# Fewer, larger transfers for sample rows, attention outputs and weight sums, and a new planned order

## The chip, the cores and the metric

The kernel runs on one core of a Trainium2 chip. The metric is device time in microseconds: 773.1 us is the median of three runs of the kernel before (771.97 to 775.28). The engines are named as in the profile: PE is TensorE (matrix products; PEld are its weight loads), DVE is VectorE, ACT is ScalarE, POOL is GpSimd, and SP is the engine that issues the transfers (DMAs).

## The reference

One layer of a streaming encoder, for 1024 prompt rows and 32 sample rows of width 1024 that share the weights:

```python
# hn = RMSNorm_pre(h)
# [qA kA vA gA qB kB vB gB] = hn @ w_in             one projection, 1024 x 4096
# oA = chunked band attention (8 heads x 64), relative-position bias
#      each frame reads its own 64-frame chunk and the previous 8 chunks
# oB = stick-breaking attention (8 heads x 64), strictly causal
# y  = concat(oA * silu(gA), oB * silu(gB)) @ w_out
# h  = h + RMSNorm_post(y)
# h  = h + sigmoid(h @ w_ple_gate) * (p @ w_ple)
```

Besides the two results it returns the new keys and values of both attentions, for prompt and sample. The sample's attention reads 512 cached rows and its own 32. All is float32.

## The kernel before

**Staging.** After a start that norms and transposes the input, eight stages follow, one for each pair of heads (A0, B0, A1, B1 and so on, A band attention, B stick-breaking). In stage n the attention of pair n is woven with the projections of pair n+1, in the last one with the gates. The pairs A1, B1, A3 and B3 carry sample attention of four heads each (`sample_attention`). Then come the embedding's products, the output product and the gate product, the latter two by a Strassen-like scheme with seven products of half matrices, which needs sums of weight quarters T1 to T4. `sum_weights` prepares these sums inside the stages 2, 4, 5 and 6 (`SUMS_AT`): for each of `o` (w_out) and `g` (w_ple_gate) and each of four row blocks it loads four quarters of 128 x 512, subtracts and adds on POOL, and stores four sums to DRAM (`sum_dr`).

**Attention of a head.** For each of eight query blocks: scores on PE into PSUM, softmax or stick-breaking weights in two tiles (`om`, `be`), and a transpose of the weights. For most blocks PE does the transpose (`ptw`). For the blocks in `ROUND` (5 to 7 of a band head, 4 to 6 of a stick-breaking head) VectorE transposes 32 x 32 squares, one transfer writes them to DRAM (`swap`) and four read them back. The result is split in a high and a low part (`wTh`, `wTl`), and every four blocks `values` multiplies them with the values into one PSUM bank (`PV`). The bank's two halves of rows are added, in two pieces of 256 columns, each through a tile `ot` and with a transfer of its own to `o_dr`.

**Keys and values.** `keys_out` and `values_out` turn a projection's columns into rows, in squares of 32 x 32, and store them as outputs. The 32 sample rows are stored by `sample_rows`, in four transfers of 4 KB for each pair and kind. `vs_dr` holds the sample's new values in squares for `sample_attention`.

**Room.** `om` and `be` tiles and some others come out of one heap of 6880 columns (`heap`), which grants room in the order in which the tiles are written down. `ot` is a ring of three tiles of 256 columns, `sg` a ring of three tiles of 512, shared by weight sums, gates and later loads.

**Order.** Nothing is issued in the order of the source. A `Recorder` keeps all operations with their dependences; `simulate` plans them with a cost for each (`cost`), `latest` gives each a due time by a backward pass, and a last `simulate` ranks each engine's queue by due time plus a shift. The shifts are two tables, `AHEAD_OF` (by engine and tile name) and `AHEAD_AT` (by stage as well). The plan models transfers by constants, and in the kernel before it lets SP issue while the pieces of transfers under way stay below 1900:

```python
            elif e == "SP":
                while away and (away[0][0] <= t or flying + o.pieces > AWAY):
                    landed, pieces = heapq.heappop(away)
                    flying -= pieces
                    t = max(t, landed)
```

All instructions are emitted from line 780, so the profile tells them apart by tile names. Every transfer is issued by SP.

Of the kernel before, what the change touches and what calls it, by code (L numbers as in the profile page):

```python
# [13 lines left out]
P = 128  # L14
D = 1024
SEQ = 1024
NS = 32
# [11 lines left out]
    ('ACT', 'L'): -809, ('ACT', 'Qfs'): -495, ('ACT', 'S'): -671, ('ACT', 'be'): 45,  # L29
    ('ACT', 'gT'): 1145, ('ACT', 'junk'): -1222, ('ACT', 'o'): 225, ('ACT', 'oT'): -1406,  # L30
    ('ACT', 'om'): -82, ('ACT', 'ot'): -967, ('ACT', 'p'): -874, ('ACT', 'pleo'): -1053,
    ('ACT', 'sgg'): 65, ('ACT', 'stq'): -314, ('ACT', 'stv'): -824, ('ACT', 'v'): 55,
    ('ACT', 'wTh'): -117, ('ACT', 'whS'): 246, ('ACT', 'whs'): 933, ('ACT', 'x'): -696,
    ('ACT', 'xS'): -616, ('DVE', 'Kl'): -588, ('DVE', 'L'): 544, ('DVE', 'S'): -85,
    ('DVE', 'Vl'): -913, ('DVE', 'cc'): -493, ('DVE', 'diags'): -1253, ('DVE', 'g'): 212,
    ('DVE', 'h'): -1097, ('DVE', 'hnl'): 570, ('DVE', 'lg'): 343, ('DVE', 'om'): -53,
    ('DVE', 'ot'): -267, ('DVE', 'over'): 483, ('DVE', 'sgg'): -356, ('DVE', 'sq'): 277,
    ('DVE', 'stats'): -1190, ('DVE', 'uu'): 246, ('DVE', 'v'): -653, ('DVE', 'vx'): -722,
    ('DVE', 'w'): -1469, ('DVE', 'wTl'): 37, ('DVE', 'wl'): 652, ('DVE', 'wlS'): -1002,
# [3 lines left out]
    ('POOL', 'be'): 196, ('POOL', 'gT'): 309, ('POOL', 'o'): -123, ('POOL', 'ogg'): 890,  # L43
    ('POOL', 'om'): 197, ('POOL', 'rs'): -497, ('POOL', 's'): -1046, ('POOL', 'sgg'): 929,
# [4 lines left out]
}  # L49
AHEAD_AT = {  # L50
    (0, 'ACT', 'pleo'): 1195, (0, 'ACT', 'sq'): 1380, (0, 'ACT', 'stk'): -1095, (0, 'ACT', 'v'): 1160,
    (0, 'DVE', 'hnl'): -45, (0, 'DVE', 'rb'): 799, (0, 'DVE', 'sq'): 461, (0, 'DVE', 'x'): 572,
# [3 lines left out]
    (2, 'ACT', 'be'): -135, (2, 'ACT', 'om'): 146, (2, 'ACT', 'stk'): -313, (2, 'ACT', 'stv'): 933,  # L56
    (2, 'ACT', 'v'): -818, (2, 'ACT', 'wTh'): 315, (2, 'ACT', 'wh'): -172, (2, 'DVE', 'S'): 534,
    (2, 'DVE', 'om'): 779, (2, 'DVE', 'wTl'): -209, (2, 'PE', 'PV'): 241, (2, 'PE', 'S'): 63,
    (2, 'PE', 'mm'): 48, (2, 'PE', 'ptw'): 89, (2, 'POOL', 'be'): -1200, (2, 'SP', 'kl'): 504,
    (2, 'SP', 'swap'): 262, (3, 'ACT', 'be'): 80, (3, 'ACT', 'om'): 256, (3, 'ACT', 'stk'): 956,  # L60
    (3, 'ACT', 'wh'): -21, (3, 'ACT', 'whs'): -356, (3, 'DVE', 'om'): -326, (3, 'DVE', 'ot'): -819,
# [3 lines left out]
    (4, 'ACT', 'om'): -35, (4, 'ACT', 'wTh'): -365, (4, 'ACT', 'whs'): -1064, (4, 'DVE', 'S'): -89,  # L65
    (4, 'DVE', 'Ss'): 1254, (4, 'DVE', 'ot'): 307, (4, 'DVE', 'wTl'): -134, (4, 'PE', 'S'): 77,
    (4, 'PE', 'ptw'): 56, (4, 'PE', 'ptws'): -349, (4, 'POOL', 'ksS'): -959, (4, 'POOL', 'om'): 162,
    (4, 'POOL', 'w'): -151, (4, 'POOL', 'wl'): 1076, (4, 'SP', 'Kcs'): 477, (4, 'SP', 'be'): -112,
    (4, 'SP', 'o'): -577, (4, 'SP', 'wr'): -890, (5, 'ACT', 'be'): -546, (5, 'ACT', 'kd'): -484,
    (5, 'ACT', 'stk'): 1450, (5, 'ACT', 'wTh'): -482, (5, 'DVE', 'S'): -110, (5, 'DVE', 'om'): -127,  # L70
# [3 lines left out]
    (6, 'ACT', 'L'): 734, (6, 'ACT', 'be'): -459, (6, 'ACT', 'kd'): 409, (6, 'ACT', 'stv'): 1412,  # L74
# [4 lines left out]
    (7, 'ACT', 'om'): 64, (7, 'ACT', 'stk'): -573, (7, 'ACT', 'wTh'): -208, (7, 'DVE', 'Kcs'): 660,  # L79
# [6 lines left out]
    (8, 'POOL', 'ogg'): -1077, (8, 'POOL', 'om'): 190, (8, 'POOL', 'sgg'): -350, (8, 'POOL', 'w'): 324,  # L86
# [3 lines left out]
    (10, 'POOL', 'r'): 153, (11, 'DVE', ''): -1125, (11, 'DVE', 'lg'): 155, (11, 'DVE', 'lo'): 1476,  # L90
    (11, 'DVE', 'ug'): -230, (11, 'DVE', 'wl'): -51, (11, 'DVE', 'wlS'): 1328, (11, 'POOL', 'h'): -525,
    (11, 'POOL', 'ms'): -252, (12, 'DVE', 'S'): 224, (12, 'DVE', 'cc'): 571, (12, 'POOL', 'gT'): -1069,
# [163 lines left out]
PASSES = 1  # L256
# [158 lines left out]
class Recorder:  # L415
# [94 lines left out]
    def cost(eng, method, args, kw, writes, reads):  # L510
# [27 lines left out]
        for v in (out, args[1]):  # L538
            if isinstance(v, View) and v.buf.pool is not None:
                size, run = 4 * v.shape[0] * v.free(), 4 * v.shape[-1]  # L540
# [82 lines left out]
    def simulate(self, rank):  # L623
# [83 lines left out]
        out, port, line, table, away, flying, last = [], 0.0, 0.0, AF.Exp, [], 0, 0.0  # L707
        while len(out) < len(self.ops):
# [26 lines left out]
            elif e == "SP":  # L735
                while away and (away[0][0] <= t or flying + o.pieces > AWAY):
                    landed, pieces = heapq.heappop(away)
                    flying -= pieces
                    t = max(t, landed)
                free[e] = t + o.busy  # L740
                line = max(line, t + DMA_START) + o.late
                heapq.heappush(away, (line + DMA_DONE, o.pieces))
                flying += o.pieces
# [42 lines left out]
def stream_step(  # L786
# [1485 lines left out]
```

## Time and profile before

| | |
|---|---|
| median of three runs | 773.1 us |
| the profiled execution, its time | 773.43 us |
| its span, first to last instruction | 771.7 us |
| busy, share of the span | PE 98%, PEld 91%, DVE 79%, ACT 68%, POOL 58% |
| mean DMA rate | 225 GB/s |
| granted clock of PE | 1.00 |

The span lies inside the execution's time; the difference is what surrounds the program. A busy share is an average over stages with different limits, so it is read by stretches. PE's ends are modelled, and short gaps between products may not show as idle time.

### The profile page before, as it was taken

Reading aid. Unit: us, or ns where it says so; the run is one execution under the profiler, and the core shown is the slowest. Engines: PE = TensorE matmul, PEld = TensorE weight load, DVE = VectorE, ACT = ScalarE, POOL = GpSimd, SP = SyncE. Lnnn points to the kernel's source line nnn. Section 1 sums busy time; section 2 is a strip of 40 time slices with the busy share of each in tenths; the row PEclk is TensorE's granted clock in tenths of the full one; section 3 lists DMA queues with packets and bytes.
Section 4 is the critical chain, followed back from the end, with each engine's and each line's share of the span. In section 5 each row is a group of like instructions: output and inputs, shape, how many; then the busy total and the mean of one; then the engine's idle time right before and its main releaser. Section 6 shows DMA issues by size and latency. Waiting matters only on the chain.

```text
span 771.7 us, 14284 instructions
## 1 busy us (share of the span) xinstructions
PE 758.4 (98%) x4410; PEld 698.9 (91%) x4410; DVE 611.6 (79%) x1067; ACT 525.0 (68%) x1122; POOL 447.2 (58%) x503
## 2 busy tenths in 40 slices
PE   9999999999999999999999999999999999999997
PEld 7999999999989899999999999999998877888786
DVE  7837868878878898959898698698565688988965
ACT  6656776787766776866788586665347877884641
POOL 6624434751356682557874467679463448689533
PEclk9999999999999999999999999999999999999999
DMA  8658667476789858889799989897779866769664
GB/s 302 220 146 223 178 166 218 120 197 206 182 192 253 218 171 229 258 237 263 216 240 269 246 231 223 270 276 214 213 267 300 275 221 227 235 202 332 214 212 136
DMA packets 202333, 173.61 MB, mean 225 GB/s; under 512 B 66817, under 2 KB 164457, under 8 KB 202258
## 3 DMA queue, kind: packets, MB, share of 16 engines
q1 hardware_dynamic: 202258, 172.70, 77.1%
q8 instruction: 35, 0.57, 0.3%
q14 instruction: 40, 0.33, 0.1%
HBM read 105.46 MB, written 58.78 MB: 213 GB/s over the span
## 4 chain that ended last, share of the span: by engine, by line
PE 86%; DVE 4%; DMA 4%; SPq 3%; issue 1%; ACT 1%; DVEq 0%; POOL 0%; ACTq 0%; POOLq 0%
PE mm_gA L780 6%; PE mm_gB L780 6%; PE mm_kA L780 6%; PE mm_qA L780 5%; PE mm_kB L780 5%; PE mm_vA L780 5%; PE mm_qB L780 4%; PE PVB L780 4%; PE mm_vB L780 4%; PE SB L780 4%; PE PVA L780 3%; PE ple L780 3%; PE SA L780 3%; SPq L780 3%; PE g0P L780 3%; PE g2P L780 3%
## 5 line engine op out<-in xcount | busy, mean ns | idle before, releaser
L780 POOL TENSOR_TENSOR be<-be 128x128 f32<-128x128 f32 (+8 forms) x66 | 85.1, 1294 | 48.6 <-DVE be L780 23.0
L780 DVE TENSOR_TENSOR_SCAN be<-be,SB 128x384 f32<-128x384 f32 (+5 forms) x96 | 91.5, 963 | 8.2 <-ACT be L780 4.3
L780 ACT ACTIVATE be<-SB 128x384 f32<-128x384 f32 (+4 forms) x192 | 83.4, 497 | 18.2 <-DVE be L780 7.0
L780 DVE TENSOR_TENSOR wTl<-be,wTh 128x640 fp32r<-128x640 f32 (+2 forms) x48 | 51.9, 1086 | 11.2 <-ACT wTh L780 7.8
L780 ACT ACTIVATE be<-be,statA 128x640 f32<-128x640 f32 (+3 forms) x64 | 44.5, 696 | 11.6 <-DVE statA L780 11.5
L780 DVE STREAM_TRANSPOSE be<-be 128x640 f32<-128x640 f32 (+3 forms) x56 | 47.9, 866 | 3.4 <-POOL be L780 2.3
L780 ACT CAST wTh<-be 128x640 fp32r<-128x640 f32 (+2 forms) x48 | 37.6, 784 | 13.2 <-DMA be<-swapB 7.3
L780 PE MATMUL SB<-kdB,LB 128*128 128x384 f32 (+5 forms) x96 | 33.7, 354 | 0.4 <-issue 0.3
L780 PE MATMUL SB<-klB,LB 128*128 128x384 f32 (+5 forms) x96 | 33.3, 347 | 0.0
L780 DVE CUSTOM_DVE_ANT_0 be<-SA,biasA 128x320 f32<-128x320 f32 (+3 forms) x64 | 29.7, 481 | 4.4 <-PE SA L780 3.4
L780 POOL TENSOR_TENSOR gB<-gB,gB 128x256 f32<-128x256 f32 x32 | 26.9, 861 | 9.8 <-DMA gB<-in_w_ple_gate_dram 7.9
L780 ACT CAST wTh<-ptwB 128x512 fp32r<-128x512 f32 (+3 forms) x48 | 22.4, 484 | 13.0 <-PE PVB L780 8.0
L780 PE MATMUL SA<-kdA,LA 128*128 128x320 f32 (+2 forms) x96 | 30.3, 325 | 0.2 <-PE mm_kB L780 0.2
L780 PE MATMUL SA<-klA,LA 128*128 128x320 f32 (+2 forms) x96 | 30.1, 317 | 0.0
L780 POOL TENSOR_TENSOR oB<-oB,oB 128x256 f32<-128x256 f32 x32 | 25.6, 826 | 6.7 <-DMA oB<-in_w_out_dram 4.8
L780 PE MATMUL ptwB<-ident,be 128*128 128x128 f32 x144 | 26.5, 274 | 2.4 <-ACT be L780 1.0
L780 POOL TENSOR_TENSOR klB<-stkB,kdB 64x1024 fp32r<-64x1024 f32 x8 | 20.0, 2504 | 14.0 <-ACT kdB L780 12.1
L780 DVE TENSOR_TENSOR wTl<-ptwB,wTh 128x512 fp32r<-128x512 f32 (+3 forms) x48 | 25.0, 540 | 3.9 <-ACT wTh L780 3.7
L780 POOL TENSOR_TENSOR klA<-stkA,kdA 64x1024 fp32r<-64x1024 f32 (+2 forms) x9 | 19.3, 2150 | 14.4 <-ACT kdA L780 9.5
L780 DVE TENSOR_TENSOR wTl<-ptwA,wTh 128x128 fp32r<-128x128 f32 (+3 forms) x48 | 21.8, 478 | 5.3 <-ACT wTh L780 3.5
L780 DVE TENSOR_TENSOR LA<-stqA,LA 64x1024 fp32r<-64x1024 f32 (+2 forms) x9 | 15.6, 1730 | 11.9 <-ACT LA L780 11.8
L780 POOL TENSOR_TENSOR wl_vB<-wr_vB,wh_vB 128x512 fp32r<-128x512 f32 x8 | 10.5, 1309 | 24.5 <-DMA stvA<-swapA 13.3
(694 smaller groups left out, 2653.6 us busy)
## 6 DMA issues: line engine op xcount, KB each, us to landing
swapA<-be SPq DMA_DIRECT2D x24, 320.0 KB, 3.7
be<-swapA SPq DMA_DIRECT2D x96, 80.0 KB, 3.0
oB<-in_w_out_dram SPq DMA_DIRECT2D x16, 256.0 KB, 4.2
sum_dro<-oB SPq DMA_DIRECT2D x16, 256.0 KB, 3.2
gB<-in_w_ple_gate_dram SPq DMA_DIRECT2D x16, 256.0 KB, 3.9
sum_drg<-gB SPq DMA_DIRECT2D x16, 256.0 KB, 3.8
x<-in_x_prompt_dram SPq DMA_DIRECT2D x16, 256.0 KB, 3.9
h_dr<-h SPq DMA_DIRECT2D x8, 512.0 KB, 4.3
```

Source lines behind the costliest of these rows:

```text
L780: getattr(getattr(tc.nc, o.what[0]), o.what[1])(*args, **kw)
```

## The change

It does the following:

- **Sample rows.** `sample_rows` stores each pair's keys as one block of squares into DRAM (`ks_dr`; the values are in `vs_dr` already). Only at the last pair of each kind does one transfer, DRAM to DRAM, gather all four pairs into the output.
- **Attention's outputs.** One copy, one addition, one transfer of 512 columns instead of two of each with 256.
- **Weight sums.** Two loads of whole rows (128 x 1024) instead of four quarters, and two stores of two sums each; the order of the sums in `sum_dr` is changed so that each pair lies together.
- **Room.** `ot` becomes two tiles of 512 columns; Qh and Ql of sample attention share one. `sg` becomes a heap of 2048 columns. The attention heap shrinks from 6880 to 6112.
- **Order.** SP's model: the next transfer is issued when the eighth before it has landed. Other constants; four backward and forward passes instead of one; both shift tables replaced in full.

Transfers: 52 fewer for sample rows, 32 for attention's outputs, 32 for weight sums.

```diff
-    ('ACT', 'L'): -809, ('ACT', 'Qfs'): -495, ('ACT', 'S'): -671, ('ACT', 'be'): 45,
+    ('ACT', ''): -789, ('ACT', 'Qs'): 1305, ('ACT', 'be'): 7, ('ACT', 'gT'): -203,
...
-ISSUE = 550
+ISSUE = 480
-DMA_START, DMA_DONE, DMA_RATE, DMA_MARGIN = 1950, 300, 320.0, 2000
-AWAY = 1900
+DMA_START, DMA_DONE, DMA_RATE, DMA_MARGIN = 1850, 1600, 320.0, 2100
+LANES = 8
-PASSES = 1
+PASSES = 4
...
-                while away and (away[0][0] <= t or flying + o.pieces > AWAY):
-                    landed, pieces = heapq.heappop(away)
-                    flying -= pieces
-                    t = max(t, landed)
+                if len(landed) >= LANES:
+                    t = max(t, landed[-LANES])
...
+    ks_dr = {ab: scratch([4, P, NS], f"ks_dr{ab}") for ab in "AB"}
-    heap = Heap(rec, at, "be", 6880)
+    heap = Heap(rec, at, "be", 6112)
+    sgs = Heap(rec, at2, "sg", 2048)
...
-    def sample_rows(dst, squares):
-        for g in range(4):
-            later(dst[:, 32 * g:32 * g + 32], squares[32 * g:32 * g + 32])
+    def sample_rows(ab, p, dst, squares, dr):
+        if squares is not None:
+            later(dr[p], squares)
+        if p == 3:
+            src = dr.rearrange("p (g t) f -> (p g) t f", t=32)
+            later(dst[0, 0].rearrange("t (p x) d -> t (p x d)", p=4).rearrange("t (x f) -> x t f", f=32), src)
...
-            for x in range(2):
-                c = slice(2 * x * P, (2 * x + 2) * P)
-                ot = at.tile([P, 2 * P], F32, tag="ot", name=f"ot{nm}_{g}_{x}", bufs=3)
-                nc.scalar.copy(ot[r], acc[o, c])
-                rec.behind()
-                nc.vector.tensor_tensor(ot[r], acc[r, c], ot[r], ALU.add)
-                dma(o_dr[sidx(ab, p)][r, (4 * g + 2 * x) * P:(4 * g + 2 * x + 2) * P], ot[r])
+            ot = at.tile([P, 4 * P], F32, tag="ot", name=f"ot{nm}_{g}", bufs=2)
+            nc.scalar.copy(ot[r], acc[o])
+            rec.behind()
+            nc.vector.tensor_tensor(ot[r], acc[r], ot[r], ALU.add)
+            dma(o_dr[sidx(ab, p)][r, 4 * g * P:(4 * g + 4) * P], ot[r])
...
-        for key in ("B12", "B22", "B11", "B21"):
-            b[key] = at2.tile([P, 512], F32, tag="sg", name=f"{w}{key}{kt}", bufs=3)
-            rec.hold(b[key])
-            dma(b[key], weight_part(w, key, kt))
...
+        for x in range(2):
+            b = sgs.tile([P, 2, 512], f"{w}B{x}{kt}", F32)
+            rec.hold(b)
+            dma(b, weight_rows(w, 4 * x + kt).rearrange("p (n c) -> p n c", n=2))
+            rows.append((b[:, 0], b[:, 1], b))
+        (b11, b12, top), (b21, b22, low) = rows
+        sub(b22, b22, b12, ALU.subtract)
+        sub(b12, b12, b11, ALU.subtract)
+        sub(b11, b22, b11, ALU.add)
+        dma(sum_dr[w][kt, 0:2].rearrange("s p c -> p s c"), top)
+        sub(b21, b11, b21, ALU.subtract)
+        dma(sum_dr[w][kt, 2:4].rearrange("s p c -> p s c"), low)
```

More of the change, by code (lines that the diff above doesn't have):

```diff
@@ L44 @@
-    ('POOL', 'om'): 197, ('POOL', 'rs'): -497, ('POOL', 's'): -1046, ('POOL', 'sgg'): 929,
[4 rows of a table removed]
+    ('ACT', ''): -789, ('ACT', 'Qs'): 1305, ('ACT', 'be'): 7, ('ACT', 'gT'): -203,
+    ('ACT', 'hnh'): -1389, ('ACT', 'junk'): -898, ('ACT', 'kd'): 1122, ('ACT', 'newh'): -1293,
+    ('ACT', 'oT'): -414, ('ACT', 'ot'): -375, ('ACT', 'pleo'): -576, ('ACT', 'sq'): -123,
+    ('ACT', 'stk'): -620, ('ACT', 'stq'): -202, ('ACT', 'stv'): -542, ('ACT', 'v'): -52,
+    ('ACT', 'vt'): -1008, ('ACT', 'w'): 293, ('ACT', 'wTh'): 73, ('ACT', 'whS'): -255,
@@ L56 @@
[L56 to L61, printed above, removed]
[3 rows of a table removed]
@@ L65 @@
[L65 to L70, printed above, removed]
[3 rows of a table removed]
@@ L92 @@
-    (11, 'POOL', 'ms'): -252, (12, 'DVE', 'S'): 224, (12, 'DVE', 'cc'): 571, (12, 'POOL', 'gT'): -1069,
[4 rows of a table added]
+    (2, 'ACT', 'be'): -228, (2, 'ACT', 'wh'): 1095, (2, 'DVE', 'S'): -256, (2, 'DVE', 'wTl'): 48,
+    (3, 'ACT', 'Kh'): -747, (3, 'ACT', 'L'): -877, (3, 'ACT', 'stk'): 463, (3, 'ACT', 'v'): 1320,
[4 rows of a table added]
+    (4, 'ACT', 'v'): -124, (4, 'ACT', 'wTh'): 148, (4, 'DVE', 'S'): 35, (4, 'DVE', 'Vl'): 65,
[6 rows of a table added]
+    (6, 'ACT', 'stq'): -1082, (6, 'ACT', 'v'): -940, (6, 'ACT', 'wTh'): 245, (6, 'DVE', 'S'): 110,
+    (6, 'DVE', 'wTl'): -591, (6, 'PE', 'S'): -57, (6, 'POOL', 'be'): -98, (6, 'POOL', 'g'): -142,
@@ new lines @@
+    (6, 'POOL', 'kl'): 171, (6, 'POOL', 'om'): 174, (6, 'SP', 'wr'): 487, (7, 'ACT', 'L'): -205,
+    (7, 'ACT', 'om'): 566, (7, 'DVE', 'Vl'): 692, (7, 'DVE', 'diags'): -616, (7, 'DVE', 'om'): -105,
[4 rows of a table added]
+    (8, 'PE', 'ptw'): -685, (8, 'PE', 'ptxs'): 106, (8, 'POOL', 'ogg'): 307, (8, 'POOL', 'om'): 622,
+    (8, 'POOL', 'sgg'): -1299, (8, 'POOL', 'wl'): 308, (8, 'SP', 'Kcs'): -265, (8, 'SP', 'Vcs'): 639,
[3 rows of a table added]
+    (11, 'ACT', 'whS'): 739, (11, 'ACT', 'x'): -201, (11, 'ACT', 'xS'): -151, (11, 'DVE', 'S'): 1275,
[4 rows of a table added]
@@ L537, in cost @@
         size, run = 4, 0
-        for v in (out, args[1]):
-            if isinstance(v, View) and v.buf.pool is not None:
+        for v in (args[1], out):
+            if isinstance(v, View) and (v.buf.pool is not None or not run):
                 size, run = 4 * v.shape[0] * v.free(), 4 * v.shape[-1]
@@ L705, in leave @@
                 come(new.place, b.gone)
-        out, port, line, table, away, flying, last = [], 0.0, 0.0, AF.Exp, [], 0, 0.0
+        out, port, line, table, landed, last = [], 0.0, 0.0, AF.Exp, [], 0.0
         while len(out) < len(self.ops):
@@ L1071, in back @@
             later(o_p[0, 0, :, h2, :].rearrange("(b p) h d -> p b (h d)", p=P), out[:, b0:8, :])
-            sample_rows(o_s[0, 0, :, h2, :].rearrange("p h d -> p (h d)"), last)
             then(out, last)
+            sample_rows(ab, p, o_s, None, vs_dr[ab])
         return [(0.1, turn), (0.0, back)]
@@ L1118, in mms @@
             if k == "g":
-                sg = at2.tile([P, 512], F32, tag="sg", name=f"sg{kind}{p}_{c}", bufs=3)[:, 0:CH]
+                sg = sgs.tile([P, 512], f"sg{kind}{p}_{c}", F32)[:, 0:CH]
                 if kind == "gA":
@@ L1239, in scores @@
                     nc.tensor.transpose(over, sums[p][0], ident)
-                    r = at.tile([P, 2 * P], F32, tag="ot", name=f"over{p}", bufs=3)[0:16, 0:P]
+                    r = at.tile([P, 2 * P], F32, tag="ot", name=f"over{p}", bufs=2)[0:16, 0:P]
                     nc.vector.reciprocal(r, over)
@@ L1496, in load_w @@
             else:
[L1497 removed]
+                raw = sgs.tile([P, 512], name, F32)
             self.raws[k, q] = raw
@@ L1884, in fetch @@
             else:
-                raw = at2.tile([P, 512], F32, tag="sg", name=f"raw{count[0]}", bufs=3)
+                raw = sgs.tile([P, 512], f"raw{count[0]}", F32)
             if count[0] < 12:
@@ L2025, in __init__ @@
             if early:
-                self.pl = at2.tile([P, 512], F32, tag="sg", name=f"pl{t}_{cols.start}", bufs=3)
+                self.pl = sgs.tile([P, 512], f"pl{t}_{cols.start}", F32)
                 self.h = fa.tile([P, 512], F32, tag="rw", name=f"hh{t}_{cols.start}", bufs=3)
```

64 lines of the change are left out of this document (20 added, 44 removed), and 63 rows, old and new, of tables (AHEAD_AT, AHEAD_OF).

## The prediction

> **What bounds the kernel now.** I read the first page, then busy time by stretch, the timeline of the transfer queue and of ScalarE around TensorE's gaps, the chain of work, and single tiles. The page first:
>
> ```profile
> span 771.7 us, 14284 instructions
> PE 758.4 (98%) x4410; PEld 698.9 (91%) x4410; DVE 611.6 (79%) x1067; ACT 525.0 (68%) x1122; POOL 447.2 (58%) x503
> PE 86%; DVE 4%; DMA 4%; SPq 3%; issue 1%; ACT 1%; DVEq 0%; POOL 0%; ACTq 0%; POOLq 0%
> ```
>
> TensorE is the bound: it is busy 98% of the span, so 13.3 us of idle time are in it. The change adds and removes no matrix product, so those 758.4 us stay, and only holes can be won. The third line (the chain by engine) says that some of the path still runs through transfers and SP's queue. Where the holes are is told by busy time in stretches of 50 us (columns: length, PE, PEld, DVE, ACT, POOL with instruction counts, granted clock, DMA share, GB/s):
>
> ```profile
> 0.00:50.00 50.00, 48.70 (x285) 44.72 (x286) 34.28 (x54) 29.87 (x59) 27.08 (x51) 1.00 0.80 256
> 150.00:200.00 50.00, 49.88 (x315) 48.31 (x315) 41.54 (x92) 36.76 (x84) 18.30 (x17) 1.00 0.70 191
> 200.00:250.00 50.00, 48.82 (x310) 46.41 (x309) 42.94 (x84) 36.63 (x80) 28.48 (x38) 1.00 0.83 213
> 250.00:300.00 50.00, 48.68 (x310) 46.30 (x308) 42.76 (x73) 37.13 (x82) 33.04 (x35) 1.00 0.75 206
> 300.00:350.00 50.00, 48.22 (x304) 45.49 (x303) 39.88 (x91) 38.24 (x86) 24.09 (x32) 1.00 0.85 240
> 350.00:400.00 50.00, 50.00 (x312) 48.48 (x311) 45.65 (x63) 37.31 (x78) 39.51 (x44) 1.00 0.86 241
> 400.00:450.00 50.00, 47.65 (x309) 45.36 (x308) 39.09 (x99) 36.03 (x84) 25.82 (x31) 1.00 0.94 243
> 450.00:500.00 50.00, 50.00 (x318) 48.67 (x317) 40.29 (x70) 34.90 (x78) 36.15 (x45) 1.00 0.91 252
> 750.00:772.00 22.00, 16.69 (x84) 13.87 (x82) 11.27 (x19) 3.79 (x7) 6.43 (x5) 0.98 0.42 140
> ```
>
> The clock is at 1.00 throughout, so it prices nothing. The start (1.30 us idle) and the end (5.31, of which 0.3 lie behind the span) hold half of the idle time, and the change touches neither. The rest lies in four stretches, 200 to 350 and 400 to 450: 1.18 + 1.32 + 1.78 + 2.35 = 6.6 us. Modelled ends hide short gaps, so I take weight loads as a second measure: in undisturbed stretches of the same mix they are busy 48.31, 48.48 and 48.67, mean 48.49; the four fall short by 2.08, 2.19, 3.00 and 3.13, together 10.4 us. What TensorE loses to waits in attention is thus 6.6 to 10.4 us, middle 8.5. That is all there is to win.
>
> What ends these waits? Around the gap near 344 us, first SP alone (start, length, what, number), then the two engines that wait:
>
> ```profile
> 337.90 0.43 SPq L780 DMA_DIRECT2D oB<-in_w_out_dram  x1
> 338.37 1.85 SPq L780 DMA_DIRECT2D be<-swapA  x4
> 340.27 0.43 SPq L780 DMA_DIRECT2D oB<-in_w_out_dram  x1
> 340.74 1.86 SPq L780 DMA_DIRECT2D be<-swapA  x4
> 342.64 0.44 SPq L780 DMA_DIRECT2D oB<-in_w_out_dram  x1
> 343.18 1.11 SPq L780 DMA_DIRECT2D o_dr<-otA  x2
> 343.49 0.73 ACT L780 CAST wTh<-be 128x640 fp32r<-128x640 f32 x1 [1.95 <-DMA be<-swapA]
> 344.72 0.30 PE L780 MATMUL ptwB<-ident,be 128*128 128x128 f32 x1 [0.87 <-ACT stvB L780]
> ```
>
> SP issues 13 transfers in 6.4 us with no pause above 0.1 us: it is full, and the loads that bring the transposed weights back queue between loads for the weight sums. ScalarE, which works in order, stands 1.95 us on such a load; the copy stvB behind it comes late, and TensorE idles 0.87 us. The chain of work in order of time says the same for another gap, and names one that isn't a transfer:
>
> ```profile
> 259.19 2.55 DVE QlsB L780
> 342.17 3.78 DMA be<-swapA
> 437.67 5.12 DMA vnsA<-vs_drA
> ```
>
> The last of these ends in the second large gap, the first in the third (TensorE's wait before SsB and before ptwA, from the waits and the timeline):
>
> ```profile
> PE SsB L780 <- DVE QlsB L780: 1.1, 1, 1.1
> 444.30 0.66 PE L780 MATMUL ptwA<-ident,be 128*128 128x128 f32 x4 [1.31 <-DVE statA L780]
> ```
>
> So of three large gaps (0.87, 1.31, 1.1) two, 2.2 of 3.3 us or 66%, go back to late transfers.
>
> **The change part by part.** What one transfer costs SP, and what one evacuation costs (duration min/median/max ns; then size and landing time in us):
>
> ```profile
> L780 ACT COPY otA<-PVA x32: 357/366/371, 82.2 to 479.0; 64x256 f32<-64x256 f32 x32
> L780 DVE TENSOR_TENSOR otA<-PVA,otA x32: 377/420/430, 82.8 to 480.4; 64x256 f32<-64x256 f32 x32
> L780 SPq DMA_DIRECT2D o_dr<-otA x32: 451/469/855, 83.3 to 481.6; - x32
> L780 SPq DMA_DIRECT2D sum_dro<-oB x16: 319/432/987, 208.7 to 365.1; - x16
> L780 SPq DMA_DIRECT2D out_dram<-ktB x32: 332/530/905, 90.4 to 508.9; - x32
> L780 SPq DMA_DIRECT2D out_dram<-vtB x20: 331/490/1617, 117.3 to 532.9; - x20
> ```
>
> *Sample rows.* Before, each of 8 key and 8 value turns issued 4 transfers: 64. After: 8 stores into ks_dr and 2 gathering copies for keys, 2 for values (their store into vs_dr existed): 12. 52 fewer, at about 0.51 (between 0.530 and 0.490; those rows mix in prompt rows): 26.5 us of SP. Nobody in the kernel reads them; the last copies fall near the last vt row, 532.9, far from the end.
>
> *Attention's outputs.* 16 heads x 2 groups x 2 halves = 64 become 32: 32 x 0.469 = 15.0 us of SP. 32 ScalarE copies and 32 VectorE additions disappear, the others have twice the columns. Their price is bounded by one and by two of the halves: 366 to 732 and 420 to 840 ns, so the two engines are relieved by 0 to 11.7 and 0 to 13.4 us. Both are off the bound (68% and 79%); I count nothing. Nor is PSUM held longer: the bank was free after one copy and two additions (1.2 us), now after one of each, at most 1.6.
>
> *Weight sums.* 8 calls x (4 loads + 4 stores) become 8 x (2 + 2): 32 fewer x 0.432 = 13.8 us. The same bytes move; GpSimd's 64 subtractions and additions stay, but the first needs both loads of twice the size (third rival).
>
> *Sum for SP:* 26.5 + 15.0 + 13.8 = 55 us out of the 500 between 50 and 550. In the stretch quoted above, 3 oB loads become 1.5 and 2 o_dr stores one: 13 transfers become 10.5, a fifth, and the queue that was full has room.
>
> *Worth on TensorE:* the 66% of 8.5 us that go back to late transfers: 5.6. Ends: 0, if what is queued otherwise comes as late, and 10.4, if the new order fills the other gaps too. I take 5.6, since the row nearest to the largest loss (343.49) shows a wait of exactly this queue. Next late thing there is VectorE's work like QlsB, which the change leaves alone.
>
> *Buffers.* ot grows from 3 x 256 to 2 x 512 columns, sg from 3 x 512 to 2048; the attention heap pays with 768 of 6880. In the forecast it costs nothing. The norm's first three x and sq tiles need 6 x 1024 = 6144, so the third sq now has to wait until VectorE has scaled the first x:
>
> ```profile
> 12.58 1.41 DVE L780 SCALAR_TENSOR_TENSOR be<-be,rs,gpre 128x512 f32<-128x512 f32 x2 [0.17 <-POOL rs L780]
> 13.88 1.08 ACT L780 ACTIVATE be<-be 128x1024 f32<-128x1024 f32 x1
> ```
>
> That ends at 13.99, ScalarE's third square starts at 13.88: 0.1 us later, beside TensorE's early embedding products. In attention, loads that come back sooner free heap sooner. If that cover is gone, it is the second rival.
>
> *New order.* PASSES, constants and both shift tables are others, so every queue is dealt anew. No row prices this. Bounds: if all ten stretches from 50 to 550 ran like the best (no shortfall), 10.4 us less; if all ran like the worst (3.13), 31 - 10.4 = 21 more. Three of the seven quoted stretches in there (150, 350, 450) run without loss by an order of the same kind, so the old order isn't poor and the new one need not be better: I take 0 and leave the ends to the range.
>
> *Sum:* the profiled execution took 773.43, its span and 1.7 around it. 773.4 - 5.6 = 767.8. It stands 0.3 above the median of the three runs, 773.1, so I forecast 767.6.
>
> **Rivals.**
>
> *1. The queue's relief is hidden.* Most of the removed transfers lie where TensorE never waits (350 to 400 and 450 to 500 are at 50.00 with DMA shares of 0.86 and 0.91, as high as in the bad stretches), so a full queue alone does not make a gap. For: exactly that pair of rows. Against: the 1.95 us at 343.49. Time: 773.
>
> *2. The heap decides, slower.* A stick-breaking head's blocks 4 to 7 take two tiles each: 2 x 128 x (5+6+7+8) = 6656 columns. That fits in 6880, not in 6112: block 7 can't be scored until block 4 or 5 has gone through its way over DRAM, which the rows below put at 0.8 + 3.7 + 3.0 + 0.7 (the cast at 343.49), about 8 us.
>
> ```profile
> L780 DVE STREAM_TRANSPOSE be<-be x56: 672/834/1112, 71.0 to 526.9; 128x640 f32<-128x640 f32 x32, 128x768 f32<-128x768 f32 x8, 128x896 f32<-128x896 f32 x8, 128x512 f32<-128x512 f32 x8
> swapA<-be SPq DMA_DIRECT2D x24, 320.0 KB, 3.7
> be<-swapA SPq DMA_DIRECT2D x96, 80.0 KB, 3.0
> ```
>
> It decides when projections run out as cover while block 7 waits. Price: one more gap of the size at 444.30 in each of the 8 such heads: 8 x 1.31 = 10.5. Time: 767.6 + 10.5 = 778.1, and 783.6 if the queue's relief fails too. Against: DVE and ACT fall short nowhere now, and projections cover most of the time. [...]
>
> *3. Coarser transfers land later.* Sizes and landing times, and GpSimd's present waits for the sums' loads:
>
> ```profile
> oB<-in_w_out_dram SPq DMA_DIRECT2D x16, 256.0 KB, 4.2
> be<-in_x_prompt_dram SPq DMA_DIRECT2D x4, 512.0 KB, 6.5
> POOL gB L780 <- DMA gB<-in_w_ple_gate_dram: 7.9, 3, 6.2
> POOL oB L780 <- DMA oB<-in_w_out_dram: 4.8, 4, 2.0
> ```
>
> A merged load is 512 KB: 6.5 instead of 4.2, 2.3 us later. GpSimd works in order, so 8 sums x 2.3 = 18 us more could stand in front of stick-breaking's products on it. If TensorE feels half, +9: 776.6. Against: GpSimd is at 58% and has to feel a wait before TensorE does; now it stands 12.7 us in 7 such waits. [...]
>
> **How the numbers follow.** Forecast 0.48, rival 1 0.20, rival 2 0.22, rival 3 0.10. A measurement of this kernel can tell about 0.5%, 3.9 us: faster means below 769.2. The forecast (its own range 763 to 771) gives 0.42 to faster and 0.06 to the same; rival 1, scattered by the new order, 0.03, 0.15 and 0.02; rival 2 0.01 to the same and 0.21 to slower; rival 3 0.03 and 0.07. Together 0.45, 0.25, 0.30. Low end 762: all 10.4 us gone (762.7), rounded for the order. High end 780: rival 2 with the relief at 778.1 and a little of the new order; left out are rival 2 at 783.6 and the worse part of the order's bound, together some 0.15, and 0.05 below.
>
> **What would show it.** Right: o_dr, sum and small out_dram issues halved or gone; in the stretches of attention weight loads at 48.3 or more everywhere, PE's idle time there below 2 us; no DMA be<-swap among the chain's pieces of 3 us and more; ScalarE's waits for be<-swap shorter. Wrong by rival 1: SP freer, but the same shortfall in weight loads, ended by VectorE or GpSimd. By rival 2: gaps that recur once in each stick-breaking head, with scores (SB) waiting for a tile's release. By rival 3: GpSimd's wait for oB and gB well above 12.7 us, with products be behind it. Wrong altogether: a shortfall before 200 us or after 550, where there is none now; then the new order made it, and no row of this profile foretold it.

## The result, and the profile after

| | before | after |
|---|---|---|
| median of 19 runs each, us | 773.1 | 777.07 |
| lowest and highest | 770.92, 775.28 | 774.1, 780.43 |
| ratio, 95% interval | | 1.0044 [1.003, 1.0059] |
| the profiled execution, us | 773.43 | 774.62 |

The kernel became 0.44% slower. The forecast was 767.6 us; the result is 9.5 us above it, and inside the range of 762 to 780. The profiled execution of after is among its faster ones. Two runs below hold one slow execution each, which counts in their medians but not in their ratios: without it the one with the sample rows left out takes 767.98 us instead of 768.73, and the last order of the second experiment 796.24 instead of 796.53.

From the first page of the kernel after: span, busy time, the chain of work by engine.

```profile
span 772.8 us, 14045 instructions
PE 756.1 (98%) x4410; PEld 699.1 (90%) x4410; DVE 610.5 (79%) x1035; ACT 522.5 (68%) x1090; POOL 452.2 (59%) x503
PE 64%; DMA 5%; DVE 3%; ACT 2%; SPq 2%; POOL 1%; issue 1%; ACTq 0%; DVEq 0%; POOLq 0%
```

As many products, 32 instructions fewer on VectorE and on ScalarE. The chain's shares can't be set beside those of before: they add up to 78% here (it can be followed back only to 172.5 us) and to 99% there. PE has 64 of the 78, that is 82%, against 87%. Busy time by stretch, kernel after (columns as before):

```profile
50.00:100.00 50.00, 48.12 (x312) 47.13 (x311) 35.61 (x79) 33.44 (x73) 18.16 (x19) 1.00 0.59 156
150.00:200.00 50.00, 48.89 (x303) 46.66 (x302) 44.26 (x75) 35.34 (x75) 21.24 (x21) 1.00 0.66 177
200.00:250.00 50.00, 47.73 (x311) 46.08 (x310) 40.81 (x90) 35.72 (x77) 28.78 (x40) 1.00 0.90 238
250.00:300.00 50.00, 48.29 (x304) 46.19 (x303) 43.32 (x66) 36.65 (x76) 28.43 (x31) 1.00 0.67 177
300.00:350.00 50.00, 48.30 (x311) 46.19 (x310) 42.55 (x92) 41.53 (x91) 24.23 (x31) 1.00 0.95 249
400.00:450.00 50.00, 49.60 (x325) 48.11 (x324) 43.30 (x98) 37.35 (x84) 29.14 (x34) 1.00 0.96 254
```

The stretch 400 to 450 is mended (47.65 before, 49.60 now; weight loads 45.36 and 48.11). But there are new holes at 50 to 100 and 150 to 200, where there was hardly one (50.00 and 49.88 before), 200 to 250 is worse (48.82 before), and 250 to 350 is as it was. TensorE's waits in the kernel after (engine, line, what it waited for: us in total, times, longest):

```profile
PE ptwB L768 <- POOL be L768: 2.8, 3, 1.6
PE PVA L768 <- DVE wTl L768: 1.9, 1, 1.9
PE ptwA L768 <- DVE wTl L768: 1.7, 1, 1.7
```

The three largest waits of before (statA, QlsB, stvB) are gone or short; others of the same size stand at other places. What lies behind the first row is told by the chain of work in order of time, kernel after, 339 to 353 us (pieces between left out at the dots):

```profile
339.42 6.79 DMA sg<-in_w_out_dram
346.35 0.73 POOL sg L768
...
348.50 1.38 POOL sg L768 x2
349.88 2.21 POOL be L768
...
352.14 0.44 PE ptwB L768 x2
```

A whole row of weights (512 KB) lands 6.79 us after its issue. GpSimd, in order, does its sums only then (346.35), and the products `be`, which TensorE's transposes wait for, come behind them (349.88). This is the third rival's mechanism, once.

### The profile page after: what moved, and what is told of

It is laid out like the page before. It is cut to its first block, busy times and chain, and to the rows that moved or that the text cites. A ratio compares the mean times of both kernels' runs of the same rounds, so it can differ in the third digit from the quotient of the medians.

```text
span 772.8 us, 14045 instructions
## 1 busy us (share of the span) xinstructions
PE 756.1 (98%) x4410; PEld 699.1 (90%) x4410; DVE 610.5 (79%) x1035; ACT 522.5 (68%) x1090; POOL 452.2 (59%) x503
## 4 chain that ended last, share of the span: by engine, by line
PE 64%; DMA 5%; DVE 3%; ACT 2%; SPq 2%; POOL 1%; issue 1%; ACTq 0%; DVEq 0%; POOLq 0%
PE mm_gB L768 6%; PE mm_gA L768 6%; PE PVB L768 4%; PE mm_kA L768 3%; PE mm_qA L768 3%; PE SB L768 3%; PE mm_kB L768 3%; PE g0P L768 3%; PE o1P L768 3%; PE g1P L768 3%; PE o3P L768 3%; PE o0P L768 3%; PE g2P L768 2%; PE o2P L768 2%; PE g3P L768 2%; PE mm_qB L768 2%
## 5 line engine op out<-in xcount | busy, mean ns | idle before, releaser
L768 POOL TENSOR_TENSOR be<-be 128x512 f32<-128x512 f32 (+8 forms) x66 | 86.8, 1321 | 45.0 <-DVE be L768 23.8
L768 ACT ACTIVATE be<-SB 128x384 f32<-128x384 f32 (+5 forms) x192 | 84.9, 498 | 29.9 <-DVE be L768 10.1
L768 DVE TENSOR_TENSOR wTl<-be,wTh 128x640 fp32r<-128x640 f32 (+2 forms) x48 | 59.8, 1248 | 4.2 <-ACT wTh L768 4.0
L768 POOL TENSOR_TENSOR sg<-sg 128x256 f32<-128x256 f32 x64 | 53.1, 854 | 6.3 <-DMA be<-swapA 2.4
L768 ACT ACTIVATE be<-be,statA 128x640 f32<-128x640 f32 (+2 forms) x64 | 44.5, 695 | 13.6 <-DVE statA L768 9.5
L768 DVE CUSTOM_DVE_ANT_0 be<-SA,biasA 128x320 f32<-128x320 f32 (+2 forms) x64 | 30.0, 481 | 4.6 <-ACT be L768 2.8
L768 POOL TENSOR_TENSOR klA<-stkA,kdA 64x1024 fp32r<-64x1024 f32 (+2 forms) x9 | 21.1, 2341 | 9.4 <-ACT kdA L768 8.7
L768 DVE TENSOR_TENSOR SB<-SB,maskb 128x128 f32<-128x128 f32 x64 | 18.0, 287 | 10.2 <-PE SB L768 9.8
L768 POOL TENSOR_TENSOR h<-h,x 128x512 f32<-128x512 f32 (+1 forms) x18 | 23.5, 1321 | 1.9 <-DVE h L768 1.9
L768 PE MATMUL ptwA<-ident,be 128*128 128x128 f32 x120 | 20.9, 274 | 2.9 <-DVE wTl L768 1.7
```

The costliest lines, as they stand in the source:

```text
L768: getattr(getattr(tc.nc, o.what[0]), o.what[1])(*args, **kw)
```

## The experiments

In several experiments the order is held: a kernel gets the list of another one's instructions for each engine, and the PSUM banks, so that only the thing named differs.

**1. The transfer queue alone, in the old order.** All else in the kernel before stays; the 64 sample-row transfers are left out, issued twice, or replaced by the change's 12.

```diff
 # left out
+    if id(o) in self.sample: continue
 # twice, the second into scratch
+    if id(o) in self.copies: tc.nc.sync.dma_start(self.copies[id(o)].get(), args[1])
 # the change's way: one store of squares into ks_dr, gathered once at the last pair (the copy stands some 30 transfers behind it)
-    later(dst[:, 32 * g:32 * g + 32], squares[32 * g:32 * g + 32])
+    rec.sample[id(o)] = dr[p], squares
+    if p == 3: rec.gather[id(o)] = whole
```

Left out:

> The kernel before, every queue in exactly its order, with the 64 transfers of sample_rows left out (the sample's new keys and values are not written; nothing else reads them). This takes 64 of the 116 transfers away without a new plan and without a smaller heap. Theory Q (TensorE's gaps come from SP's full queue, as predicted): 64/116 of the forecast 5.6 us, so about 3.1 us faster, ratio 0.996. Theory O (the queue's length does not decide; gaps come from the order, from buffers and from engines that work in order): within 0.2%, ratio 0.998 to 1.002.

Measured: 768.73 us, ratio 0.9949 [0.9929, 0.9969]. Twice:

> The kernel before in exactly its order, with each of the 64 transfers of sample_rows issued twice, the second into scratch memory right behind the first: 64 more transfers, some 32 us more of SP's time. Theory Q: the queue is full between 300 and 500 us, so these push loads back by several us in all; 3 us or more slower, ratio 1.004 to 1.015. Theory O: within 0.3%.

Measured: 783.35 us, ratio 1.014 [1.0114, 1.0165]. The change's way:

> The kernel before with the change's way for sample rows alone (keys by one store into scratch, values by the store that is there, one gathering copy DRAM to DRAM for each of the four outputs), every other instruction in exactly the order of before, its tables and its heap of 6880: 52 transfers fewer, nothing left out. Theory Q (queue load decides, order kept): 52/64 of what leaving 64 out gave (0.51%), so 0.4% faster, ratio 0.994 to 0.998. If the gain there came from the bytes or the small pieces that were not written, rather than from the transfers: within 0.2%.

Measured: 769.94 us, ratio 0.997 [0.9948, 0.9992]; it is complete and beats both kernels. Busy time by stretch with the transfers left out, 300 to 350 and 400 to 450:

```profile
300.00:350.00 50.00, 49.18 (x316) 47.60 (x316) 41.24 (x90) 39.77 (x91) 25.75 (x35) 1.00 0.84 242
400.00:450.00 50.00, 50.00 (x331) 48.56 (x330) 42.53 (x108) 40.05 (x93) 27.48 (x35) 1.00 0.94 253
```

The two gaps that the prediction put down to the full queue are smaller or gone (48.22 and 47.65 before). So the queue makes TensorE's holes: that step holds, in one order, and its size too. 64 transfers fewer gave 3.9 us where the prediction's 5.6 us for 116 make 3.1, and the change's 52 fewer gave 2.3 where they make 2.5. It isn't even, though: 64 more cost 10.8 us.

**2. Orders without shift tables.** Both tables emptied; then the old and new plan, heap and transfers combined.

```diff
-AHEAD_OF = { ... }
-AHEAD_AT = { ... }
+AHEAD_OF = {}
+AHEAD_AT = {}
 # and in some: heap 6112 in the kernel before; LANES, constants and PASSES of the other plan
```

> The kernel before with both shift tables empty, so that the plan's due times alone order the queues. If the tables carry much of the speed (theory T): 5 to 15 us slower than before, 778 to 788. If they are polish: within 3 us.

> The changed kernel with both shift tables empty. Theory T: slower than with them by 5 us or more. Beside the run without tables of the kernel before it compares structure and plan model without tables: if the larger transfers and the eight counted places help by themselves, it is 3 us or more faster than that one; if the smaller heap (6112 instead of 6880) eats the gain, equal or slower.

> The kernel before with the new plan model (eight places, new constants, four passes) and empty tables; transfers and heap as before. If the model of eight places helps by itself, faster than the kernel before without tables (779.7) by 2 us or more, about 776. If the larger transfers are what made the changed kernel without tables the faster one (777.3 against 779.7), then 779 or more.

> The kernel before with empty tables and the attention heap cut from 6880 to 6112, nothing else. Theory H (the heap's cut costs what the transfers gain): 4 us or more slower than the same with 6880 (779.7), so 784 or more. If the heap is no matter: within 2 us of it.

> The kernel before with the new plan model, empty tables and the heap of 6112: all of the change but its larger transfers. Theory H: 4 us or more slower than the new model with 6880. The larger transfers' own worth is the step from here to the changed kernel without tables (777.3); theory Q says 5 us or more, so 782 or more here.

> The kernel after with the old plan (old constants, old model of the transfer queue, one pass) and both tables empty. It stands to the run of the kernel before with empty tables and the small heap (785.0 us) as the larger transfers alone, and to the kernel after with empty tables (777.3) as the plan alone. If larger transfers are worth 11 us in any untuned order and the new plan costs 4: 773 to 774 us, which is better than the kernel after as it stands. If the two can't be added, because each new order is a fresh draw with a scatter of some 4 us: anywhere from 770 to 781, and 777 most likely. If the new plan only fits the changed transfers (it costs with the old ones and pays with the new): above 779.

| transfers | heap | plan | us | ratio, 95% interval |
|---|---|---|---|---|
| old | 6880 | old | 779.73 | 1.0091 [1.0068, 1.0114] |
| old | 6880 | new | 784.39 | 1.0144 [1.0104, 1.0183] |
| old | 6112 | old | 785.0 | 1.0157 [1.0125, 1.019] |
| old | 6112 | new | 788.7 | 1.0199 [1.016, 1.0238] |
| new | 6112 | new | 777.31 | 1.0063 [1.0041, 1.0086] |
| new | 6112 | old | 796.53 | 1.0299 [1.0262, 1.0335] |

With the new plan the larger transfers (with their rooms) are worth 788.7 - 777.3 = 11.4 us, with the old plan they cost 796.5 - 785.0 = 11.5. The expected price of the smaller heap (784 or more) and worth of the larger transfers (782 or more without them) came out, but the last row gives the same transfers the opposite sign. So the table can't be read as a sum of parts: these orders scatter by more than any part of the change. The kernel before has tables that gain 6.6 us (779.7 to 773.1); those of the kernel after gain 0.2 (777.3 to 777.1).

**3. Tables fitted anew.** Two new tables, fitted by as many random trials to the old plan alone, for the changed and for the unchanged transfers.

```diff
-AHEAD_OF = {}
-AHEAD_AT = {}
+AHEAD_OF = { ... }   # 155 and 571 entries for the changed transfers, 152 and 554 for the old ones
+AHEAD_AT = { ... }
 # for the changed transfers also the old plan's constants, its model of the transfer queue and one pass
```

> The kernel after with the old plan (constants, model of the transfer queue, one pass), which took 796.5 us with empty tables, and two new tables fitted to that plan alone by some 12,700 trials of random shifts. If tables fitted to the plan carry over to the chip: 775 to 782 us. If the time of an order is a fresh draw whatever the plan thinks of it: anywhere from 777 to 797.

> The kernel before, old plan and heap, but its two tables replaced by others, fitted to the same plan alone by some 12,800 random trials. With its own tables it takes 773.1 us, with none 779.7. If fitting to the plan carries over: 772 to 775. If it doesn't, and the kernel's own tables are worth their 7 us only because they suit the chip: 778 to 784 us, or more. Theory O needs the second, or something near it: an equally good plan may lose several us on the chip.

Measured: changed transfers 774.35 us, ratio 1.0012 [0.9994, 1.003]; old transfers 774.83 us, 1.0023 [0.9999, 1.0047]. Fitting carries over to the chip in both, and with equal fitting the two sets of transfers can't be told apart. Each is one fit; with its own tables and with these the kernel before differs by 1.7 us (773.1 and 774.8). The kernel after as it stands lies 2.7 us above its own transfers in a better order.

**4. The smaller heap.** First in the old order: the kernel before with 6112 columns, each engine as before except where a tile has no room. In the first run the PSUM banks were dealt anew as well, in the second they were kept.

```diff
+        place = {id(o): n for n, o in enumerate(out)}
+        for heap in self.heaps: heap.cols = min(heap.cols, ROOM)     # ROOM = 6112
+        return self.simulate(lambda o: (0, place[id(o)], o.index), banks)[0]
```

> The kernel before, its own order, and one thing changed: the attention heap has 6112 columns. Each engine keeps the old order of its queue except where a tile has no room any more: 34 of 4410 products, 28 of 1021 ScalarE instructions, 9 of 967 VectorE, 19 of 498 GpSimd and 3 of 970 transfers come later than others that they preceded. Theory H (the smaller heap itself costs about 4 to 5 us, as between the untuned orders, 779.7 to 785.0): 777 to 778 us, ratio 1.005 to 1.007, and longer waits of GpSimd's memset be than the 9.8 us of before. Rival (prediction: the heap costs nothing, and the difference of the untuned orders was the scatter of orders): 772 to 774, ratio 0.999 to 1.001. Prediction's second rival (one gap in each stick-breaking head): 783.

> The kernel before with a heap of 6112 columns once more, in its own order, now with each PSUM tile in the bank that it has there (in the run of 822.5 us the banks were dealt anew, too). Theory H: the time stays at 815 to 825 us and ScalarE's waits to reuse a tile that a transfer still reads stay near 43 us. Rival (the banks, not the heap, made most of the 49 us): under 790 us.

Measured: 822.54 us, 1.0641 [1.0615, 1.0667], and 818.78 us, 1.0584 [1.0557, 1.061]. The banks thus made little of it. The group of ScalarE's waits that is the largest with 6112 columns, first in the kernel before, then with 6112 columns and the banks kept:

```profile
ACT be L780 <- DMA swapB<-be: 0.9, 1, 0.9
```

```profile
ACT be L812 <- DMA swapB<-be: 54.7, 16, 8.5
```

In the old order a heap of 6112 columns, its tiles laid out anew by first fit, costs 45 us, far outside the 772 to 783 expected of the first run: ScalarE stands 54.7 us, in 16 waits, before writing a tile whose room a transfer still reads. How much of it is the size and how much the layout isn't separated; no layout fitted to the old order was tried for 6112 columns. With the room as it is dealt here, the change could not keep its order.

Then in the new order, with the kernel after's list and banks. First the heap got 6880 columns again, laid out by first fit; then with a layout fitted to the order, with a control, and the layout alone.

```diff
-    heap = Heap(rec, at, "be", 6112)
+    heap = Heap(rec, at, "be", 6880)
-    hnl = [hnp.tile(...) for c in range(NCH)]
+    hnl = [hnp.tile(...) for c in range(NCH - 1)]
+    hnl.append(hnl[1])
+            if self.known: b.lo = self.known[self.next]     # the fitted layout
 # with more room and in its control: the last third's low part isn't written
+                if c < NCH - 1:
                     nc.vector.tensor_tensor(hnl[c][dst], sv, f(hnh[c][dst]), ALU.subtract)
```

> The kernel after, each engine's queue in the order that it has there and every PSUM bank dealt as there, but the attention heap has 6880 columns again. The room comes from the low part of the normed input's last third, which shares a tile with the second third's (the products that read it get other values; as many instructions as before; 16 products and 8 ScalarE instructions of the start move behind others). Theory H (what the change loses, it loses in the smaller heap): the waits for a tile's release, 18.5 us on ScalarE and GpSimd in the kernel after and 8.7 in the kernel before, fall to 9 or less, TensorE's waits ptwB behind GpSimd's be (2.8 us) and PVA behind wTl (1.9) go, and the time is 769 to 772 us, ratio 0.995 to 0.999, as low as the fixed old order with gathered sample rows. Theory O (the order itself has its gaps, which the heap does not end): the waits for release fall, but the time is 775 to 778 us, ratio 1.003 to 1.007. Half of each: 773 to 774.

> The kernel after in its exact order and banks, with an attention heap of 6880 columns whose tiles are laid out anew so that a tile reuses room that has been free for longer (by the order's own spacing; in the run of 797.7 us the layout fell out by first fit). The room comes from leaving out the low part of the normed input's last third (7 VectorE subtractions of the start; the products read the second third's instead). Theory H (the smaller heap makes the change's gaps): the waits for release fall from 18.5 us to under 9, TensorE's waits for them go, and the time is 769 to 772 us, 4 to 7 below the run with the same left out and the old layout. Theory O (the order itself): the waits fall, the time stays within 2 us of that run. Theory L (this order has been fitted to one layout of the heap, and any other one hurts): above 780 us, as before.

> Control for the run with more room: the same instructions left out (the low part of the normed input's last third), the kernel after's own order, banks, heap of 6112 columns and layout. It should take what the kernel after takes, or a little less by its start: 774 to 777 us, ratio 1.001 to 1.006. If it takes 780 or more, leaving these out isn't neutral and the run of 797.7 us told nothing on the heap.

> The kernel after complete, in its exact order and banks, its heap still of 6112 columns, only the tiles' places in it laid out anew (longer free before reuse). Theory H: the waits for release fall a little and the time with them, 774 to 777 us. Theory O: 776 to 778. Theory L (order and layout belong together): above 780.

Measured: first fit 797.69 us, 1.0328 [1.03, 1.0356]; more room in the fitted layout 777.73 us, 1.0055 [1.0034, 1.0076]; its control 777.19 us, 1.005 [1.0032, 1.0068]; the layout alone 778.8 us, 1.0064 [1.0041, 1.0087]. The waits for a tile's release, kernel after, ScalarE and GpSimd:

```profile
ACT be L768 <- DVE wTl L768: 3.2, 4, 1.0
ACT be L768 <- DMA swapA<-be: 2.1, 3, 1.3
ACT be L768 <- PE ptwB L768: 0.9, 1, 0.9
ACT be L768 <- DMA swapB<-be: 0.4, 1, 0.4
POOL be L768 <- DMA swapA<-be: 5.1, 3, 2.6
POOL be L768 <- DMA swapB<-be: 2.2, 1, 2.2
POOL be L768 <- DVE wTl L768: 1.8, 2, 1.0
POOL be L768 <- PE ptwA L768: 1.6, 1, 1.6
POOL be L768 <- PE ptwB L768: 1.2, 2, 0.8
```

Together 18.5 us. The same rows with more room:

```profile
ACT be L821 <- DVE wTl L821: 2.8, 2, 2.0
ACT be L821 <- DMA swapB<-be: 1.9, 2, 1.6
POOL be L821 <- DVE wTl L821: 1.0, 1, 1.0
```

5.7 us are left, and the time is that of the control. In the new order more room gains nothing that can be measured: theory H, which wanted 4 us or more, falls. (A new layout by itself took 778.8 us against 777.1, so a gain below 2 us could be hidden.) The 797.7 us of the first fit lie outside every expectation, and it wasn't the room, as the run with the same room in the fitted layout shows. Whether the layout made them, or the tile that two thirds then shared, no run separates. The trace points to the layout: ScalarE waits 20.0 us before `be` for transfers out of `swapB`, in five waits (0.4 in the kernel after), the same wait as with 6112 columns in the old order.

**5. All larger transfers in the old order.** The kernel after's transfers and its rooms for `ot` and `sg`, with the order, banks and heap layout (6880) of the kernel before.

```diff
-    heap = Heap(rec, at, "be", 6112)
+    heap = Heap(rec, at, "be", 6880)
+PLACES = "..."   # the order of the kernel before; a merged instruction at the place of its first part, a merged store at its last
+BANK_OF, LOWS = ...   # its banks and heap layout; the last third's low part left out, as in the fourth experiment
```

> Every larger transfer of the change (sample rows, attention's outputs, weight sums, 116 fewer in all, with the change's rooms for ot and sg), but in the order, PSUM banks and heap layout of the kernel before, heap of 6880 columns. A merged instruction stands where the first of its parts stood, a merged store of outputs or sums where the last did. The room comes from leaving out the low part of the normed input's last third (7 VectorE subtractions; neutral in the kernel after, 777.2 against 777.1 us). 4 products, 1 ScalarE, 3 VectorE, 1 GpSimd instruction and 8 transfers stand elsewhere than before. Theory O (the transfers help and the new order loses it): 764 to 769 us, ratio 0.988 to 0.995; the sample rows alone gave 769.9, and all three free twice as much of the transfer queue. Rival R (rows and outputs help, merged sums or outputs hurt by landing later): 771 to 776. Rival (transfers of the change as a whole hurt): above 777.

Measured: 796.26 us, ratio 1.0305 [1.0276, 1.0335]. The last of the rivals holds: the merged outputs and sums, with their rooms, together cost 796.3 - 769.9 = 26 us in this order (no run separates the two). Busy time by stretch in this run:

```profile
250.00:300.00 50.00, 49.01 (x308) 46.33 (x308) 43.90 (x72) 37.01 (x80) 31.97 (x35) 1.00 0.77 206
300.00:350.00 50.00, 44.70 (x273) 42.83 (x272) 35.91 (x79) 35.27 (x74) 21.65 (x30) 0.94 0.84 235
```

Up to 300 us it runs as well as before (48.68 there); from then on it breaks. The first large hole, at 344 us, comes from the room `ot`. Its three tiles became two, and they serve not only the outputs but also `over` (reciprocals that VectorE computes) and `Qs` of sample attention. Three of TensorE's four largest waits in this run:

```profile
PE SsA L821 <- ACT QsA L821: 5.1, 1, 5.1
PE SB L821 <- DVE over L821: 4.8, 1, 4.8
PE SB L821 <- DVE sg L821: 3.9, 1, 3.9
```

Around the second of them, the piece of the chain of work and then TensorE:

```profile
341.20 3.47 DMA o_dr<-otA
345.70 0.64 PE L821 MATMUL SB<-kdB,LB 128*128 128x320 f32 x1 [4.78 <-DVE over L821]
```

VectorE starts `over` at 344.70, when the store of outputs has landed (344.67), after 4.98 us of waiting, and TensorE stands 4.8 us behind it. Before `QsA` the chain shows such a store too (`o_dr<-otA`, from 444.49, 4.75 us). The fourth wait comes from the sums: SP's queue, then ScalarE and TensorE:

```profile
369.77 0.43 SPq L821 DMA_DIRECT2D sum_dro<-sg  x1
376.30 0.35 SPq L821 DMA_DIRECT2D sg<-in_w_ple_gate_dram  x1
376.69 4.79 SPq L821 DMA_DIRECT2D be<-swapB  x9
381.13 0.73 ACT L821 CAST wTh<-be 128x640 fp32r<-128x640 f32 x1 [5.33 <-issue]
385.86 1.65 PE L821 MATMUL PVB<-wTh,v2B 128*128 128x512 f32 x3 [3.40 <-ACT wTh L821]
```

And the two pieces of the chain of work that are sums' transfers there:

```profile
369.77 6.51 DMA sum_dro<-sg
376.30 4.39 DMA sg<-in_w_ple_gate_dram
```

SP issues a store of sums at 369.77 and then stands 6.1 us, until the store has landed at 376.28, before it issues the next row's load into the same room. Nine loads that attention needs queue behind it; ScalarE stands 5.33 us and TensorE 3.40. The room for sums grew from 1536 to 2048 columns, but it holds two tiles where it held three, and a call of `sum_weights` needs both: the next call's load can't start ahead. The wait for `sg` above is of the same room: a gate's tile, which ScalarE writes, stands 2.8 us for a store of sums. So four waits, 5.1 + 4.8 + 3.4 + 3.9 = 17.2 us, go back to the two rooms. Beside the run with the gathered sample rows TensorE idles 18.3 us more (797.6 - 767.4 = 30.2 against 768.6 - 756.7 = 11.9) and takes 10.7 us longer for the same products, at a lower clock (0.92 to 0.97 in the stretches from 300 to 550 us; see the last section).

## Why the prediction was wrong

- **TensorE is the bound, only holes can be won.** Right for the kernel before and after (busy 98% of the span in both): the products are unchanged, and the difference is in the holes. Where long holes came, clock was lost too: 10.7 of the 29.0 us between the profiled executions of the fifth experiment's run and of the one with gathered sample rows (797.6 and 768.6) are longer products.
- **What the transfers cost SP (55 us).** Right: summed over the traces, SP issues 854 transfers in 434.5 us where it issued 970 in 488.1, 53.6 us less. 32 stores `o_dr` at the same 0.469 us each are left. The share of the sample rows was too high, though: replacing them alone saves SP 17.2 us, not 26.5.

```profile
L768 SPq DMA_DIRECT2D o_dr<-otA x16: 451/469/2442, 83.2 to 483.9; - x16
```

- **Worth on TensorE, 5.6 us.** The mechanism is shown where the order is held: 64 transfers fewer, 0.51% less; 64 more, 1.4% more; the change's own sample rows, 0.3% less. For the other 64 of the 116 transfers the step failed: merged, they don't only relieve the queue.
- **Buffers: nothing.** This is the first step that failed. It counted columns (`ot` 3 x 256 to 2 x 512, `sg` 1536 to 2048), not tiles, three of which became two, and in its sum it took the heap to be a question of the first tiles only. In the old order the merged tiles with their rooms cost 26 us, against a relief of 2 to 4; 17.2 us of TensorE's waits there go back to the rooms. The smaller heap, laid out by first fit, costs 45 in that order.
- **New order: I take 0.** This is the second, and it decides the sum. The prediction added the relief to an order that stays as good as it was. But the change's rooms, as tried, don't fit the old order, so a new one had to win back tens of us, and the gain that was forecast belonged to the old one. Fitted alike, both sets of transfers end at 774.4 and 774.8 us: no relief is left that shows beside the 1.7 us between two sets of tables for the kernel before. The order that the kernel after comes with lies 2.7 us above that. Which of its shifts makes the holes at 95 and 346 us wasn't tried.
- **Rival 1 (relief hidden, 773).** 4 us below the result, and wrong in its reason: where the order is held, the queue's relief does reach TensorE (3.9 us without the sample rows, 2.3 with them gathered).
- **Rival 2 (the heap).** Its wait is seen in the old order (ScalarE, 54.7 us in 16 waits, up to 8.5 us each, at four times the price in all), with the layout as a second possible cause. It is not seen in the new order, where no gap recurs in each stick-breaking head; that its 778.1 us lies only 1 us from the result is luck.
- **Rival 3 (coarser transfers land later).** Its 776.6 us is the nearest of all, but only in part for its reason. The 512 KB loads land in 6.4 and 5.4 us, near the 6.5 that it took. But GpSimd's waits for them fell to 3.7 us, from 12.7:

```profile
POOL sg L768 <- DMA sg<-in_w_out_dram: 2.2, 2, 1.5
POOL sg L768 <- DMA sg<-in_w_ple_gate_dram: 1.5, 1, 1.5
```

 One such load stands in front of the largest group of TensorE's waits (346 us, above). The 3.7 us leave it out, since GpSimd's wait there, 2.36 us, is put down to another transfer (`be<-swapA`).
- **What would show it.** "A shortfall before 200 us: then the new order made it": it came, in the stretches 50 to 100 and 150 to 200, and the gap near 95 us stays at 1.9 us when the same order gets more room. That no row of the old profile foretold the place is true. That the order would have to be another one could be read from the diff, where the number of tiles stands.

## What to carry to other kernels

When transfers are merged, count the tiles that a room holds, not its columns: in the fifth experiment's run a load that had to wait for the last store out of the same room held SP's queue for 6.1 us, with nine loads behind it. Where an order is planned, a gain that was read from the old order's gaps holds only if the old order can be kept, so ask first whether it still fits into the room. Take the part that needs no room: the sample rows alone gave 0.3%, the whole change lost 0.44%.

## What the runs showed of the hardware

The prediction said that the clock prices nothing. It does, at times. TensorE's gap near 95 us is the same 1.9 us in the profiled executions of the run with more room and of its control. Busy time there, first with more room, then the control (granted clock is the third column from the end):

```profile
93.50:97.00 3.50, 1.57 (x9) 1.24 (x9) 2.51 (x3) 2.46 (x4) 2.86 (x3) 0.95 0.84 239
97.00:100.50 3.50, 3.50 (x15) 3.31 (x15) 1.46 (x3) 0.85 (x2) 1.43 (x3) 0.56 0.76 183
```

```profile
93.50:97.00 3.50, 1.62 (x11) 1.30 (x10) 2.75 (x3) 2.70 (x6) 2.62 (x3) 1.00 0.76 226
97.00:100.50 3.50, 3.50 (x24) 3.42 (x24) 1.67 (x3) 0.85 (x2) 1.60 (x2) 1.00 0.81 196
```

In the one the clock fell to 0.56 for the next 3.5 us, and 15 products ran where 24 did in the other: the gap cost 3.5 x (1 - 15/24) = 1.3 us more, two thirds of its own length. A longer gap was followed by a lower clock too, 0.50 for 5 us. In the fifth experiment's run, behind TensorE's wait of 4.8 us:

```profile
345.00:350.00 5.00, 4.30 (x15) 4.24 (x16) 3.95 (x8) 1.87 (x4) 3.84 (x6) 0.50 0.56 112
```

From 300 to 550 us that run's stretches of 50 us were granted 0.94, 0.92, 0.97, 0.96 and 0.97, which falls short by 50 x (0.06 + 0.08 + 0.03 + 0.04 + 0.03) = 12 us; its products took 10.7 us longer. So part of what the long holes of this run cost is clock. By its granted clock the run with more room falls short by 3.5 x (0.05 + 0.44) = 1.7 us at its gap of 1.9 us. The kernel after has a gap of 1.88 us at the same place, and was granted 1.00 behind it like the control: why one of the three gaps was followed by a lower clock, no run shows.
